# Joint semaphores for pairs of GpSimd and ScalarE pieces in a row maximum that ignores NaN

## The chip, the cores and the metric

The kernel runs on one NeuronCore of a Trainium2 chip. The metric is the device time of one execution in microseconds (us). The executions of one kernel in one set of rounds spread over 0.16 to 0.75 us here, so differences of half a us can be read if several runs are taken; each comparison with the kernel before uses runs of the same chip and rounds. All runs were with a granted clock (the share of full clock that the chip allows) of 1.00.

## The reference

The input is 32 x 2048 x 2048 floats, about a tenth of them NaN. The result is the maximum of each row of 2048, NaN left out.

```python
def reference(x, axis):          # axis = -1
    return np.nanmax(x, axis=axis).astype(np.float32)
```

That is 537 MB to read and 0.26 MB to write.

## The kernel before

The data flows through four stages. SyncE (SP) issues loads of a tile (7 rows of 2048 floats in each of 128 partitions) into one of three buffers `xt`. ScalarE (ACT) makes 16-bit keys `kt` of the upper halves of the floats. GpSimd (POOL) turns keys back into upper halves that are no longer NaN and writes them into `xt`; for some pieces ScalarE does this itself (a "back" piece, a negative number in the list of tiles). VectorE (DVE) takes the maximum of each row. When VectorE is done with a buffer, its next load is issued.

A tile's plan is a triple: sizes of loads, of pieces, and of reductions, in quarters of a row:

```python
    + [([28], [7, 9, 12], [16, 12])] * 7
    + [([28], [9, 12, -7], [8, 20])]          # the last 7 quarters are cleaned by ScalarE
...
    + [([4, 4, 3, 2, 4, 2, 3, 3, 3], [2, 2, 4, (-2.0, 1), 2, 3, 3, (-1, 2), (1, -1, 1), 2, -1.0], [4, 4, 4, 4, 4, 4, 4])]
```

There are 74 tiles. The order between engines is kept by hand. Each engine counts its instructions on one semaphore of its own; an instruction that depends on others waits for their counts. In this program an instruction carries one wait; each further one becomes an instruction of its own ahead of it:

```python
    def add(self, who, engine, issue, deps, lane=None, step=1):
        want = self.needed(who, deps)
        for s, v in want[:-1]:
            engine.wait_ge(self.sems[s], v)         # an instruction of its own
        inst = issue()
        for s, v in want[-1:]:
            inst._wait_ge(self.sems[s], v)          # on the instruction itself
        name = lane or who
        inst.then_inc(self.sem(name), step)
        self.count[name] += step
        event = (name, self.count[name])
        self.past[event] = {**self.seen[who], name: event[1]}
        return event
...
    e = dve([e for a, b, e in clean if b > lo and a < done] + part,
            nc.vector.tensor_reduce, ...)           # a row maximum: waits for POOL, or for POOL and ACT
```

A reduction whose quarters were cleaned partly by GpSimd and partly by ScalarE so has two waits: an instruction on VectorE's sequencer (EVENT_SEMAPHORE in the trace), then the reduction. VectorE has 18 such extra waits in the whole program, and the trace shows 18 EVENT_SEMAPHORE records just before reductions, of 21 ns each.

## Time and profile before

| | before |
|---|---|
| device time, median of 6 runs (range) | 1253.72 us (1253.66 to 1253.86) |
| DMA queue of the loads, share of 16 engines' span | 99.3% |
| VectorE, ScalarE, GpSimd busy | 89%, 79%, 93% |
| separate waits of VectorE before reductions | 18 |
| landing of the last load (its data complete) | 1243.20 us |

The prediction shows the lines that say what bounds the kernel.

The timeline of the tail before (start us, length us, engine, line, operation, count, idle time before it and who ended it):

```profile
1233.78 1.15 ACT L187 ACTIVATE kt<-xt,scalars 128x1024 uint16<-128x1024 int16 x1 [0.33 <-DMA xt<-in_x_dram]
1237.89 8.42 POOL L191 TENSOR_SCALAR xt<-kt 128x1536 int16<-128x1536 uint16 x6 [0.95 <-ACT kt L187]
1239.84 8.87 DVE L195 TENSOR_REDUCE acc<-xt 128x1 f32<-128x2048 f32 x4 [0.50 <-POOL xt L191]
```

Read it downwards: ScalarE waited 0.33 us for a load, GpSimd then 0.95 us for ScalarE, and VectorE 0.50 us for GpSimd. After that VectorE has four row maxima to do without a pause, and the end follows 12.0 us after 1239.84 us.

### The profile page before, as it was taken

How to read it: one execution, taken by the hardware profiler on the slowest of the kernel's cores; microseconds unless marked ns; L12 is line 12 of the kernel's file. 1: busy time of each engine (PE TensorE's matmuls, PEld its weight loads, DVE VectorE, ACT ScalarE, POOL GpSimd, SP SyncE). 2: the span in 40 equal slices, each digit the busy share in tenths (PEclk: the TensorE clock that was granted, in tenths of full speed). 3: DMA queues.
4: the chain of work that ended last, by engine and by line, in shares of the span. 5: the costliest groups of instructions: out<-in, count | busy, mean ns of one | idle time of the engine just before them, and what ended most of it. 6: DMA issues, size and time to landing. Idle time of an engine off the chain costs nothing.

```text
span 1251.8 us, 892 instructions
## 1 busy us (share of the span) xinstructions
DVE 1110.9 (89%) x181; ACT 986.9 (79%) x273; POOL 1168.4 (93%) x242
## 2 busy tenths in 40 slices
DVE  0788989888889988898988888998888899999998
ACT  3777887778787877788777877777777878999998
POOL 2999989998999899998999899999999999989997
DMA  9999999999999999999999999999999999999997
GB/s 415 436 418 436 440 440 436 422 433 440 440 434 423 433 440 440 436 425 429 440 440 438 425 427 440 440 438 429 423 440 440 435 434 421 437 428 431 431 428 288
DMA packets 15991, 537.20 MB, mean 429 GB/s; under 512 B 2544, under 2 KB 2544, under 8 KB 3568
## 3 DMA queue, kind: packets, MB, share of 16 engines
q1 hardware_dynamic: 15984, 537.14, 99.3%
q14 instruction: 7, 0.06, 0.0%
HBM read 536.87 MB, written 0.26 MB: 429 GB/s over the span
## 4 chain that ended last, share of the span: by engine, by line
DMA 36%; DVE 33%; POOL 19%; ACT 10%; SPq 1%; issue 1%; DVEq 0%
DMA xt<-in_x_dram 36%; DVE acc L195 33%; POOL xt L191 19%; ACT kt L187 9%; ACT xt L187 1%; SPq L253 1%; DVE none L201 0%; DVE acc L215 0%; SPq L411 0%; DVEq L124 0%; SPq L183 0%
## 5 line engine op out<-in xcount | busy, mean ns | idle before, releaser
L191 POOL TENSOR_SCALAR xt<-kt 128x3584 int16<-128x3584 uint16 (+11 forms) x236 | 1167.4, 4946 | 78.5 <-ACT kt L187 60.3
L195 DVE TENSOR_REDUCE acc<-xt 128x3 f32<-128x6144 f32 (+4 forms) x175 | 1107.7, 6380 | 137.1 <-POOL xt L191 129.2
L187 ACT ACTIVATE kt<-xt,scalars 128x3584 uint16<-128x3584 int16 (+9 forms) x247 | 935.5, 3825 | 257.8 <-DMA xt<-in_x_dram 241.8
L187 ACT ACTIVATE xt<-kt 128x512 int16<-128x512 uint16 (+6 forms) x24 | 52.8, 2200 | 0.7
L187 ACT ACT_TABLE_LOAD x1 | 1.3, 1283 | 0.9 <-SPq L183 0.9
L195 DVE TENSOR_REDUCE xt<-xt 128x1 f32<-128x1536 f32 x1 | 1.7, 1742 | 0.0
L221 DVE MEMSET scalars<- 128x1 f32 x1 | 0.1, 59 | 1.0 <-SPq L183 1.0
L201 DVE TENSOR_SCALAR none<-acc 128x414 int32<-128x414 f32 (+1 forms) x2 | 0.8, 380 | 0.1
L215 DVE TENSOR_TENSOR acc<-acc,none 128x414 int32<-128x414 int32 (+1 forms) x2 | 0.7, 374 | 0.1
L201 POOL TENSOR_SCALAR late<-acc 128x91 int32<-128x91 f32 x1 | 0.5, 545 | 0.1
L215 POOL TENSOR_TENSOR acc<-acc,late 128x91 int32<-128x91 int32 x1 | 0.3, 343 | 0.1
L397 POOL MEMSET const-float32-0.0<- 128x1 f32 x1 | 0.1, 98 | 0.2 <-issue 0.2
L187 ACT ACTIVATE scalars<-scalars 128x1 f32<-128x1 f32 x1 | 0.2, 203 | 0.0
L397 POOL MEMSET const-uint8-127<- 128x1 uint8 x1 | 0.1, 102 | 0.0
L397 POOL MEMSET const-bfloat16-1.0<- 128x1 bf16 x1 | 0.1, 101 | 0.0
L397 POOL MEMSET const-float32-1.0<- 128x1 f32 x1 | 0.1, 98 | 0.0
## 6 DMA issues: line engine op xcount, KB each, us to landing
xt<-in_x_dram SPq DMA_DIRECT2D x61, 7168.0 KB, 22.5
xt<-in_x_dram SPq DMA_DIRECT2D x2, 5120.0 KB, 17.3
xt<-in_x_dram SPq DMA_DIRECT2D x3, 2816.0 KB, 22.5
xt<-in_x_dram SPq DMA_DIRECT2D x4, 2048.0 KB, 22.1
xt<-in_x_dram SPq DMA_DIRECT2D x5, 1536.0 KB, 28.9
xt<-in_x_dram SPq DMA_DIRECT2D x2, 3584.0 KB, 24.5
xt<-in_x_dram SPq DMA_DIRECT2D x6, 1024.0 KB, 26.7
xt<-in_x_dram SPq DMA_DIRECT2D x3, 1792.0 KB, 29.8
```

The source lines that it names most:

```text
L187: return order.add("act", nc.scalar, lambda: nc.scalar.activation(**kw), deps)
L191: "pool", nc.gpsimd, lambda: nc.gpsimd.tensor_scalar(**kw), deps
L195: return order.add("dve", nc.vector, lambda: do(**kw), deps)
L201: lambda: engine.tensor_scalar(out=none, in0=acc, scalar1=NONE, scalar2=float(0x00800000), op0=ALU.is_equal, op1=ALU.mult,),
L215: lambda: engine.tensor_tensor(out=bits, in0=bits, in1=none, op=op),
L221: e_top = order.add("dve", nc.vector, lambda: nc.vector.memset(top, EDGE), [])
L253: lambda: nc.sync.dma_start(out=xt[:, at : at + c], in_=xg[:, base + at : base + at + c]),
L397: nc = _bacc.Bacc("TRN2", target_bir_lowering=False, num_devices=1)
```

## The change

The last GpSimd piece and the last ScalarE piece that one reduction needs now count on a semaphore of that pair. The reduction waits for the value 2 of it, in one wait on itself. The core of the diff:

```diff
+APART = (70, 71, 72, 73)                    # tiles left as they were
...
+def joints(pieces, reds):                   # which pieces form a pair of one reduction
+    ...
+    for need in needs:
+        if len(need) == 2 and all(sum(i in n for n in needs) == 1 for i in need):
+            for i in need:
+                pairs[i] = tuple(need)
+    return pairs
...
-    def add(self, who, engine, issue, deps, lane=None, step=1):
+    def add(self, who, engine, issue, deps, lane=None, step=1, joint=False):
...
-        self.past[event] = {**self.seen[who], name: event[1]}
+        past = self.past.get((name, event[1] - step), {}) if joint else {}
+        self.past[event] = {**past, **self.seen[who], name: event[1]}
...
-        def act(deps, **kw):
-            return order.add("act", nc.scalar, lambda: nc.scalar.activation(**kw), deps)
+        def act(deps, pair=None, **kw):
+            return order.add("act", nc.scalar, ..., deps, lane=pair, joint=pair is not None)
... (the same for pool)
+                pairs = {}
+                if number not in APART:
+                    pairs = joints(pieces, [n // Q for n in reds])
...
+                def name(i):
+                    return f"pair{number}_{pairs[i][0]}" if i in pairs else None
```

In the two programs every tile operation stands in the same place. VectorE has 10 separate waits fewer (tiles 9, 17, 25, 33, 41, 63, 66, 67, 68, and one in tile 74, the last), ScalarE has 4 more.

More of the change, by code (lines that the diff above doesn't have):

```diff
@@ L77, in total @@
     return sum(sum(map(abs, p)) if isinstance(p, tuple) else abs(p) for p in pieces)
+def joints(pieces, reds):
+    flat = []
+    at = 0
+    for step, parts in enumerate(pieces):
+        for c in parts if isinstance(parts, tuple) else (parts,):
+            flat.append((at, at + abs(c), c < 0, step + isinstance(c, float)))
+            at += abs(c)
+    needs = []
+    done = 0
+    for n in reds:
+        over = [i for i, (a, b, _, _) in enumerate(flat) if a < done + n and b > done]
+        done += n
+        pools = [i for i in over if not flat[i][2]]
+        backs = [i for i in over if flat[i][2]]
+        if pools and backs and flat[pools[-1]][3] > flat[backs[-1]][3]:
+            backs = []
+        needs.append(pools[-1:] + backs[-1:])
+    pairs = {}
[4 more added lines that the diff above has]
+    return pairs
 class Order:
@@ L184, with pool @@
         order = Order(nc)
-        def act(deps, **kw):
-            return order.add("act", nc.scalar, lambda: nc.scalar.activation(**kw), deps)
-        def pool(deps, **kw):
+        def act(deps, pair=None, **kw):
             return order.add(
-                "pool", nc.gpsimd, lambda: nc.gpsimd.tensor_scalar(**kw), deps
+                "act",
+                nc.scalar,
+                lambda: nc.scalar.activation(**kw),
+                deps,
+                lane=pair,
+                joint=pair is not None,
+            )
+        def pool(deps, pair=None, **kw):
+            return order.add(
+                "pool",
+                nc.gpsimd,
+                lambda: nc.gpsimd.tensor_scalar(**kw),
+                deps,
+                lane=pair,
+                joint=pair is not None,
             )
@@ L225, with last @@
         kfree = [[] for _ in range(NKEYS)]
+        clock = 0
+        def last(uses):
+            return list({back: e for back, _, e in sorted(uses, key=lambda u: u[1])}.values())
         key = 0
@@ L269, with cleaned @@
                 held = []
+                pairs = {}
+                if number not in APART:
+                    pairs = joints(pieces, [n // Q for n in reds])
+                flat = sum((p if isinstance(p, tuple) else (p,) for p in pieces), ())
+                half = {}
+                piece = 0
+                def cleaned(a, b, k, i, e):
+                    nonlocal clock
+                    clock += 1
+                    both = [(a, b, k, flat[i] < 0, clock)]
+                    if i in pairs:
+                        if pairs[i] not in half:
+                            half[pairs[i]] = both
+                            return
+                        both += half.pop(pairs[i])
+                    for a, b, k, back, when in both:
+                        kfree[k].append((back, when, e))
+                        clean.append((a, b, e))
+                def name(i):
+                    return f"pair{number}_{pairs[i][0]}" if i in pairs else None
                 def release():
-                    for a, b, k, kp, e in held:
+                    for a, b, k, kp, e, i in held:
                         e = act(
                             [e],
+                            name(i),
                             out=xt[:, a:b].bitcast(i16)[:, 1::2],
@@ L280, in release @@
                         )
-                        kfree[k].append(e)
-                        clean.append((a, b, e))
+                        cleaned(a, b, k, i, e)
                     held.clear()
@@ L292 @@
                         used = 0
-                        kold, kfree[key] = kfree[key], []
+                        kold, kfree[key] = last(kfree[key]), []
+                        assert all(k != key for q in half.values() for _, _, k, _, _ in q)
                         if at + c == sum(loads) * Q:
-                            kold = kold + kfree[(key + 1) % NKEYS]
+                            kold = kold + last(kfree[(key + 1) % NKEYS])
                     e_key = act(
@@ L313 @@
                         if back:
-                            held.append((at - c, at, key, kp, e_key))
+                            held.append((at - c, at, key, kp, e_key, piece))
                             if not wait or at == sum(loads) * Q:
@@ L319 @@
                                 [e_key],
+                                name(piece),
                                 out=to,
@@ L326 @@
                             )
-                            kfree[key].append(e)
-                            clean.append((at - c, at, e))
-                        while reds and done + reds[0] <= min([at] + [h[0] for h in held]):
+                            cleaned(at - c, at, key, piece, e)
+                        piece += 1
+                        open_ = [h[0] for h in held] + [p[0] for q in half.values() for p in q]
+                        while reds and done + reds[0] <= min([at] + open_):
                             n = reds.pop(0)
```

## The prediction

> **What bounds the kernel now.** I read the page's counts first (part 1), then the slices (part 2), then the chain that ended last, then single records of the trace around the reductions that have two waits.
>
> ```profile
> DVE 1110.9 (89%) x181; ACT 986.9 (79%) x273; POOL 1168.4 (93%) x242
> DMA  9999999999999999999999999999999999999997
> q1 hardware_dynamic: 15984, 537.14, 99.3%
> HBM read 536.87 MB, written 0.26 MB: 429 GB/s over the span
> ```
>
> No compute engine is full, although GpSimd (POOL) is near it. The DMA engines are: 99.3% of 16 engines' span, a 9 in every slice but the last. The busy-time view of stretches says the same without the start and the tail:
>
> ```profile
> 20.00:1236.00 1216.00, 1096.03 (x172) 973.26 (x261) 1155.96 (x229) 1.00 1.00 433
> 1040.00:1236.00 196.00, 195.51 (x52) 188.53 (x76) 184.23 (x55) 1.00 1.00 429
> 1236.00:1252.00 16.00, 12.53 (x8) 10.14 (x10) 9.84 (x9) 1.00 0.40 155
> ```
>
> (Columns: stretch, its length, DVE, ACT, POOL, clock, DMA share, GB/s.) From 20 to 1236 us the DMA share is 1.00 and 433 GB/s come in. From 1040 us VectorE is full as well, 195.51 of 196 us, so there I have to ask which of the two sets the end. The chain that ended last answers it:
>
> ```profile
> 1213.18 23.03 DMA xt<-in_x_dram
> 1236.21 0.03 issue
> 1236.24 1.58 ACT kt L187
> 1237.82 0.07 issue
> 1237.89 1.92 POOL xt L191
> 1239.81 0.03 issue
> 1239.84 2.01 DVE acc L195
> 1241.84 0.20 issue
> 1242.04 2.06 DVE acc L195
> 1244.10 0.13 issue
> 1244.23 2.15 DVE acc L195
> 1246.38 0.05 issue
> 1246.42 2.29 DVE acc L195
> ```
>
> (Start us, length us, what.) A load of 1 MB issued at 1213.18 lands 23.03 us later, though at 429 GB/s its own bytes take 2.4 us: it stands behind some 20 us of earlier loads. So its landing at 1236.21 is set by bytes and rate, not by the moment VectorE freed a buffer. After it come one key (ACT), one clean (POOL), four row maxima on VectorE, two tiny fix-ups and the store. The end is therefore **the stream, to 1236.2 us, plus a tail of 15.6 us** (1251.8 - 1236.2). A change of waits can only gain in that tail, or lose by letting the stream run dry.
>
> [...] the two-wait reductions have an EVENT_SEMAPHORE record on VectorE's sequencer just before them, the others have none. [...] Where POOL ended last and VectorE was ready, a one-wait reduction started 35 ns after POOL's end (1239.801 to 1239.836). A two-wait reduction, whose separate wait was POOL's, started 103, 103, 110 and 107 ns after (at 1065.339, 1140.913, 1237.048, 1246.424): 38 ns to the EVENT_SEMAPHORE, then about 70 ns for the instruction behind it. The price of the second wait, when the one that ends last is the separate one, is thus **about 70 ns**. [...]
>
> **The change part by part.** Comparing the order of instructions of the two programs, every tile operation stands in the same place with the same size; only waits differ. On VectorE 10 of 18 separate waits go: one each in tiles 9, 17, 25, 33, 41, 63, 66, 67, 68, and one in the last tile. Three other pairs of the last tile keep two waits, because a third piece of their row still counts on POOL's own semaphore (the pair's event does not carry POOL's earlier count). On ACT nothing is removed, and four keys (tiles 63, 66, 67, 68) now wait for POOL and for the pair: four separate waits added. Tiles 70 to 73 are left out by the list in the source.
>
> 1. *Tiles 9 to 41 (5 waits).* The reductions start at 158.50, 293.83, 429.06, 564.60, 699.86, each 32 to 33 ns after ScalarE's clean and 439 to 466 ns after POOL's. One line shows it:
>
> ```profile
> 158.50 10.82 DVE L195 TENSOR_REDUCE acc<-xt 128x5 f32<-128x10240 f32 x1 [1.54 <-ACT xt L187]
> ```
>
> The separate wait (POOL) had been over for 400 ns; the reduction sat at its own wait. Gain 0.
>
> 2. *Tiles 63, 66, 67, 68 (4 waits).* Back to back, reductions of VectorE start some 80 to 90 ns ahead of the recorded end of the one before. Those of tiles 66 and 67 (1110.625, 1125.678) start 90 and 87 ns before that end: full pace, gain 0. Those of 63 and 68 (1065.339, 1140.913) start 103 ns after POOL's end, and 68 and 33 ns after the previous reduction's end: gain about 70 ns each, 0.14 us together. But this frees buffers earlier in a stretch where the DMA share is 1.00, so it shortens a queue, not the stream. On the path: 0.
>
> 3. *Last tile.* The third row's reduction (1237.048) starts 38 ns before the previous end instead of 82: its early wait would now be an older piece (POOL ended it at 1235.522) and the pair's wait sits on the instruction, so it gains 45 ns. The next one waits 0.50 us for POOL anyway (1239.84), and swallows it. Of the last three, at 1242.039, 1244.231, 1246.424, each starts 82 to 84 ns before the recorded end of its predecessor, the back-to-back pace: start to start 2.19 us. Their separate waits opened inside that time. Even the last, where POOL and ACT both ended at 1246.317 and 107 ns passed, coincides with the pace to 1 or 2 ns. Gain on the path: 0 to 0.002 us.
>
> 4. *ACT's four added waits.* At some 60 to 70 ns each if they are the last to open, at most 0.28 us, spread over tiles at 1060 to 1150 us where ACT is busy 188.53 of 196 us; it has 7 us of slack there, and the load queue of 20 us lies beyond. On the path: 0.
>
> Sum: 0.00 us of the tail, 0.00 of the stream; **1253.66 us**, the median of before less the 2 ns.
>
> **Rivals.** (a) *Every removed wait counts*: 10 x 0.07 = 0.7 us, 1253.0 us. For it speaks that VectorE is full from 1040 us on; against it the records above, where only three of the ten or so waits cost anything, and the 20 us of queued loads. (b) *The tail gains*: if in other executions POOL or ACT ends the last rows a little later than in this one, up to 3 x 0.07 = 0.2 us of the four last reductions could be won, 1253.45 us; the last row stands right at the edge, so a few tens of ns are plausible. (c) *ACT's extra waits or the additional semaphores delay a key that feeds POOL*, and POOL comes late in the tail: at most 0.3 us, 1253.95 us; against it, the last tile has no added wait on ACT and ACT waited for DMA data at 1233.78 and 1236.24, so delays are wiped out there.
>
> **Range and chances.** The three runs of before lie within 0.20 us, and its profiled run took 1253.59. Rivals (b) and (c) are a few tenths either way, and another session may shift both kernels by some tenths: I take 1253.2 to 1254.0. Two per cent are 25 us. That would need the stream to slow or stop, and no wait here is worth more than a tenth of a us: same 0.99, 0.005 to either side.
>
> **What would show it right or wrong.** Right: DMA share 1.00 to 1236 us again, last landing at 1236.2 within some tenths, VectorE's last four reductions 2.19 us apart, the reductions at 1065 and 1141 starting about 35 ns after POOL's end and not 103, total idle of VectorE before reductions unchanged but for tenths. Wrong: a last landing that moves by over 0.5 us, an idle DMA stretch near the four changed keys, or a new gap between the last four reductions.

No term of the sum goes with them; it came to 0.00 us of the tail and 0.00 of the stream, so 1253.66 us. That the stream cannot bring more rests on the measured DMA share of 1.00, at 433 GB/s, alone; that 433 GB/s is its limit is not shown.

## More of the kernel before

One view is the DMA view of a short stretch. This is the one of 1231 to 1233 us, near the end of the stream of loads (queue and kind, then packets, MB, share of 16 engines):

```profile
q1 hardware_dynamic: 169, 0.86, 104.4%
q14 instruction: 1, 0.01, 1.0%
```

(A packet counts whole in the stretch in which it starts, so a share can pass 100%.) Queue 1 brings the data. Queue 14, labelled "instruction", is read here as the program itself.

## The result and the profile after

| | before | after |
|---|---|---|
| device time, median of 6 runs (range) | 1253.72 (1253.66 to 1253.86) | 1253.22 us (1253.08 to 1253.31) |
| recorded instructions | 892 | 886 |
| idle of VectorE before and between its last eight reductions | 0.50 us | 0 |
| last instruction fetch in the trace | 1231.70 us | 1245.68 us |

The ratio of the two is 0.9996, with a 95% interval from 0.9983 to 1.0009 (ratios are the mean time of one kernel's runs over that of the other's of the same rounds, so not quite the ratio of these medians). By that interval the kernels are the same within 2%, as forecast. That interval contains 1. But the ranges of the runs do not overlap, and they did not on the two later chips where both kernels ran: 16 runs of the changed kernel lie between 1253.07 and 1253.39, all 31 runs of the kernel before, in four sets of rounds, between 1253.44 and 1254.01. So there is a gain of about **0.5 us**, 0.04%, that the prediction's sum does not contain.

The parts of the page are all but the same:

```profile
span 1251.4 us, 886 instructions
DVE 1110.7 (89%) x181; ACT 986.6 (79%) x273; POOL 1168.6 (93%) x242
q1 hardware_dynamic: 15984, 537.14, 99.3%
```

The stretches, in the same columns as in the prediction, also: DMA share 1.00, 433 GB/s, and VectorE full from 1040 us.

```profile
20.00:1236.00 1216.00, 1095.74 (x172) 973.33 (x262) 1155.84 (x229) 1.00 1.00 433
1040.00:1236.00 196.00, 195.45 (x52) 188.82 (x77) 184.35 (x55) 1.00 1.00 429
```

And the line of tile 9, where the prediction saw no gain, answers as it should: the reduction still waits for ScalarE, and as long.

```profile
158.32 10.82 DVE L243 TENSOR_REDUCE acc<-xt 128x5 f32<-128x10240 f32 x1 [1.55 <-ACT xt L226]
```

The difference is in the tail. The timeline after:

```profile
1230.67 17.63 DVE L243 TENSOR_REDUCE acc<-xt 128x1 f32<-128x2048 f32 x8
1237.47 8.41 POOL L236 TENSOR_SCALAR xt<-kt 128x1536 int16<-128x1536 uint16 x6 [0.27 <-ACT kt L226]
```

VectorE now runs eight reductions without a pause; its 0.50 us of idle time is gone. So is ScalarE's wait for the load, and GpSimd waits 0.27 us instead of 0.95. The waits of the last tile did not do this: the load itself arrived earlier. The landings in the two traces show it (us; loads numbered from 0, the last is 104):

```
load            98        99       100       103       104
before     1231.77   1233.76   1236.21   1241.08   1243.20
after      1232.02   1233.27   1235.70   1240.66   1243.15
```

Up to load 98 the changed kernel is 0.25 us *later* (the times of one kernel's six runs spread over about as much, 0.20 us before and 0.23 us after). From 98 to 99 the kernel before takes 1.98 us, the changed one 1.24. The pause of 0.74 us before load 99 falls where its instruction packet stands, at 1231.70. In the changed kernel this stretch has no such packet:

```profile
q1 hardware_dynamic: 169, 0.87, 104.1%
```

It comes later, in the DMA view of 1233 to 1250 us, at 1245.68 by the trace, after the last load has landed:

```profile
q1 hardware_dynamic: 1523, 3.70, 54.8%
q14 instruction: 1, 0.01, 0.2%
```

In both traces VectorE had started 189 recorded instructions at that moment. With 10 instructions fewer, VectorE starts its 189th at 1244.50 us in place of 1230.42.

How do 0.74 us of a late load become 0.5 us of time? VectorE has some slack: in three traces with the packet before load 99 (before, and e1 and e3 below) the load is 0.74, 0.92 and 0.97 us late (against 1.24 us after load 98), and VectorE idles 0.50, 0.72 and 0.76 us. And more than this idle time cannot be won there, because without it VectorE works from 1141 us to the end with no pause over 0.04 us:

```profile
1141.21 80.59 DVE L243 TENSOR_REDUCE acc<-xt 128x3 f32<-128x6144 f32 x26
1221.71 1.75 DVE L243 TENSOR_REDUCE xt<-xt 128x1 f32<-128x1536 f32 x1
1223.49 24.81 DVE L243 TENSOR_REDUCE acc<-xt 128x1 f32<-128x513 f32 x12
```

The end of the changed kernel therefore no longer hangs on the last loads.

### The profile page after: what moved, and what is told of

Read it like the earlier page. It is cut to its first block, busy times and chain, and to the rows that moved or that the text cites. A ratio compares the mean times of both kernels' runs of the same rounds, so it can differ in the third digit from the quotient of the medians. Undisturbed runs are those within 1.5% of the kernel's fastest.

```text
span 1251.4 us, 886 instructions
## 1 busy us (share of the span) xinstructions
DVE 1110.7 (89%) x181; ACT 986.6 (79%) x273; POOL 1168.6 (93%) x242
## 3 DMA queue, kind: packets, MB, share of 16 engines
q1 hardware_dynamic: 15984, 537.14, 99.3%
## 4 chain that ended last, share of the span: by engine, by line
DMA 38%; DVE 29%; POOL 20%; ACT 12%; issue 1%; SPq 0%; ACTq 0%
DMA xt<-in_x_dram 38%; DVE acc L243 29%; POOL xt L236 20%; ACT kt L226 11%; ACT xt L226 1%; SPq L307 0%; DVE none L249 0%; DVE acc L263 0%; SPq L491 0%; ACTq L158 0%; SPq L219 0%
```

## The experiments

The theory after this comparison, the **fetch theory**: the removed waits gain nothing as waits. They gain as *instructions*: with fewer of them VectorE's next 8192 bytes of program are fetched behind the stream of loads instead of inside it. Rivals: the **wait theory** (one wait instead of two gains in the last tile) and the **buffer theory** (reductions of tiles 63 and 68 start earlier, free buffers earlier, and the stream gains). All experiments gave correct results.

### Parts of the change, alone

`e1`: pairs in the last tile only. `e2`: pairs in the nine earlier tiles only.

```diff
-APART = (70, 71, 72, 73)
+APART = tuple(range(1, 74))            # e1
+APART = (70, 71, 72, 73, 74)           # e2
```

> Pairs in the last tile alone; VectorE has 1 separate wait fewer than before, ScalarE none more. Fetch theory (the 0.5 us come from an 8192-byte instruction fetch of VectorE that moved from 1231.7 us, inside the stream of loads, to 1245.7 us, behind it, because VectorE has 10 instructions fewer): the fetch comes back to some 1231 to 1240 us and the time is about 1253.6. If the fetch has moved to 1237 or later by that one instruction, part of the gain stays. Wait theory (the gain is the cheaper wait in the last rows): 1253.2.

> Pairs in the nine earlier tiles, none in the last tile; VectorE has 9 separate waits fewer, ScalarE 4 more. Fetch theory: fetch at 1240 us or later, time 1253.2 to 1253.3. Wait theory: the last tile's waits are those of before, so 1253.7. Buffer theory (buffers freed earlier in tiles 63 and 68 speed the stream): 1253.2.

On one chip, kernel before 1253.62 us (7 runs): e1 took **1253.90** (1253.61 to 1254.04, 4 runs), e2 **1252.94** (1252.82 to 1253.08, 4 runs). The part with the last tile's cheaper waits gains nothing; the part without them has the whole gain. The wait theory has fallen. (Both times lie some 0.3 us outside what the fetch theory expected, e1 above and e2 below. In e1's profiled run, its slowest, load 99 is later than in the kernel before, and VectorE idles 0.72 us; for e2 see e9.) In e1 the fetch stands at 1231.96 us and load 99 lands 2.16 us after load 98; in e2 the fetch stands at 1246.76, load 99 follows after 1.24 us, and VectorE's last eight reductions have no idle time.

### The instructions back, with nothing else

`e3`: the changed kernel, with all its pairs, plus ten waits on VectorE for a count reached long before, one in each of tiles 43 to 52, where VectorE has idle time (in the kernel before it is busy for 16.5 to 18.3 of each 20 us from 720 to 900 us). `e4`: the same ten in the kernel before.

```diff
                             n = reds.pop(0)
+                            if done == 0 and 43 <= number < 53:
+                                nc.vector.wait_ge(order.sems["dve"], 1)
```

> The changed kernel with all its pairs and ten waits put into VectorE's stream, one in each of tiles 43 to 52, each on a count reached long before, where VectorE idles anyway. Fetch theory: VectorE's count of instructions is that of before again, the fetch is back near 1231.7 us and the time near 1253.65. Wait theory and buffer theory: all pairs are there, 1253.2.

> The kernel before with the same ten waits added. Fetch theory: the fetch comes ten instructions earlier, near 1205 us, still in the stream; time 1253.5 to 1254.0 if a fetch anywhere in the stream delays all later landings, about 1253.2 to 1253.4 if it only hurts among the last few loads. Wait and buffer theory: 1253.7.

Same chip and rounds: e3 took **1253.68** us (1253.62 to 1253.78, 4 runs), the level of the kernel before; e2, which has the pairs of the nine earlier tiles and no idle waits, took 1252.94. (The changed kernel itself was not run on this chip.) Its DMA view of 1231 to 1233 us has the packet again (the trace says 1232.04),

```profile
q1 hardware_dynamic: 167, 0.87, 105.5%
q14 instruction: 1, 0.01, 1.0%
```

and its tail has the old waits again:

```profile
1233.97 1.15 ACT L226 ACTIVATE kt<-xt,scalars 128x1024 uint16<-128x1024 int16 x1 [0.53 <-DMA xt<-in_x_dram]
1238.07 8.42 POOL L236 TENSOR_SCALAR xt<-kt 128x1536 int16<-128x1536 uint16 x6 [1.14 <-ACT kt L226]
1240.01 8.87 DVE L243 TENSOR_REDUCE acc<-xt 128x1 f32<-128x2048 f32 x4 [0.76 <-POOL xt L236]
```

The ten waits cost nothing by themselves: up to load 98 the landings of e3 are 0.29 us earlier than in the changed kernel. Load 99 then lands 2.21 us after 98. This undoes the gain while every pair stays, which neither rival allows.

e4 took **1253.69** us (1253.54 to 1254.29, 4 runs). Its fetch came earlier, at 1218.59 us (the expectation had said near 1205), and so did the pause: loads 91 to 92 now take 3.22 us instead of 2.43 in the changed kernel, and loads 98 to 99 only 1.24. A fetch 13 us earlier in the stream therefore costs about the same: counted from load 91, loads 92 to 103 stay 0.6 to 0.8 us later than in the changed kernel. Only the very last load catches up.

### A part that opens no wait earlier

`e5`: pairs in tiles 9, 17, 25, 33 and 41 only. The prediction showed that their separate waits had opened 400 ns before; ScalarE gets no extra wait here.

```diff
-APART = (70, 71, 72, 73)
+APART = tuple(range(60, 75))
```

> Pairs in tiles 9, 17, 25, 33 and 41 alone: five of VectorE's separate waits fewer, none of which had opened last, and no wait added anywhere. Fetch theory: the fetch goes to about 1242 us or later, so the whole gain is there, 1252.9 to 1253.3. Wait theory and buffer theory: 1253.65, as not one reduction starts earlier by it.

`e6`: the changed kernel with five idle waits on VectorE (`43 <= number < 48` in the edit of e3).

> The changed kernel with five of the ten idle waits put back on VectorE (tiles 43 to 47). Fetch theory: the fetch request falls at about 1236 to 1239 us, so it delays at most the last two to four loads: 1253.1 to 1253.6, between the two kernels. Wait and buffer theory: 1253.2.

`e7`: the changed kernel with ten idle waits on SP, in the same tiles:

```diff
                 at = 0
+                if 43 <= number < 53:
+                    nc.sync.wait_ge(order.sems["dve"], 1)
                 for c in loads:
```

> The changed kernel with ten such waits on the queue engine (SP) in place of VectorE, in the same tiles. Fetch theory, with VectorE's own count as the cause: VectorE's fetch stays at about 1245 us, 1253.2. If any ten instructions on any engine do it: 1253.65.

`e8`: the changed kernel, unedited, on the same chip.

> The changed kernel itself on this chip, to compare e5 to e7 with it in the same rounds: 1253.1 to 1253.25 by every theory. e5 may come out below it by up to 0.3 us if the four waits added on ScalarE cost something.

The four ran in the same rounds; the kernel before took 1253.71 us (1253.44 to 1254.01, 9 runs).

| run | VectorE's wait instructions, against before | time, us (5 runs each) | last fetch, us |
|---|---|---|---|
| e5 | -5 | 1253.36 (1253.06 to 1253.43) | 1243.11 |
| e6 | -5 | 1253.42 (1253.25 to 1253.86) | 1239.74 |
| e7 | -10, SP +10 | 1253.24 (1253.16 to 1253.42) | 1245.88 |
| e8 | -10 | 1253.16 (1253.11 to 1253.32) | 1245.63 |

e5 has most of the gain, 0.35 us, although not one of its reductions starts earlier by its pair; its runs and those of the kernel before just miss each other (1253.43 and 1253.44). Its fetch falls 0.09 us before the last load lands, and VectorE has no idle time in the tail. Its time lies 0.06 us above the range expected and 0.20 above e8; why is not shown. This is against the buffer theory as well. e6 is between, as expected, and its runs overlap those of the kernel before: its fetch falls before the last two landings, load 103 lands 2.68 us after 102 (1.84 in the changed kernel), and the profiled execution, its slowest with 1253.86 us, ends on that load. The chain that ended last starts there:

```profile
1220.31 21.42 DMA xt<-in_x_dram
1241.74 0.02 issue
1241.76 1.58 ACT kt L226
```

e7 separates the engines. Ten instructions more on SP leave the time and VectorE's fetch as they are. They move another packet, from 1130 us to 1055 us: in both traces SP had then started 80 or 81 recorded instructions. So the last packet follows VectorE's count, and this one SP's.

One packet does not follow so simple a rule. In the kernel before, e1 and e4 it comes at 434 us; in every run without the five early waits it comes at 386 us, although VectorE has fewer instructions ahead of it (47 started in the changed kernel, 56 in the kernel before). Why is not shown. Tile 25's separate wait opens at 428.64 us in the kernel before, 5.6 us ahead of the packet; no run tests whether the two are connected. This packet is not the cause of the gain: in e3 it stands at 386 us as in the changed kernel, and the gain is gone.

### Is there a better version?

`e9`: e2 again. `e10`: the changed kernel again. `e11`: pairs in tiles 9 to 41 and in the last, so that ScalarE gets no extra wait (`APART = (63, 66, 67, 68, 70, 71, 72, 73)`).

> Pairs in the nine earlier tiles, none in the last, once more, beside the changed kernel in the same rounds. It was 0.68 us under the kernel before where the changed kernel was 0.50 under it, but on two chips. Fetch theory: the two have the fetch behind the stream alike, so they lie within 0.2 us of each other. If the pairs of the last tile cost something, this one is 0.2 us or more below.

> The changed kernel on this chip: 1253.1 to 1253.3 by every theory.

> Pairs in tiles 9 to 41 and the last tile: six separate waits fewer on VectorE, none added on ScalarE. Fetch theory: the fetch comes at about 1242 to 1245 us, behind all loads that the end hangs on: 1253.0 to 1253.3. If the four waits added on ScalarE in the changed kernel cost time, this one lies below it.

Kernel before 1253.72 us (1253.54 to 1253.86, 9 runs). e9 took 1253.19 (1253.06 to 1253.61), e10 1253.17 (1253.07 to 1253.39), e11 1253.16 us (1252.99 to 1253.39), 5 runs each: no difference. The larger gain of e2 in the first set, 0.68 us, did not come again on this chip, where e9 gains 0.53. The four waits added on ScalarE cost nothing that shows, and no version was found that beats the changed kernel.

## Why the prediction was right or wrong

The time, 1253.22 us, lies just inside the stated range, 1253.2 to 1254.0, and "within 2%" was right. The point given, 1253.66 us, was 0.44 us too high. That the range still held was luck: its tenths were meant for rivals (b) and (c) and for a shift between sessions, none of which happened. Of its own signs, two of being right came true (the reductions at 1065 and 1141 us start 34 and 32 ns after GpSimd's end, and the last four start 2.19 us apart), and one of being wrong did by a hair: the landing that it called the last moved by over 0.5 us, from 1236.21 to 1235.70. By its steps:

- **What bounds the kernel**: right for the kernel before. The DMA share and the rate are the same after, but in the changed kernel's trace the end hangs on VectorE, which no longer waits. One sentence of it was wrong: that the landing at 1236.21 us "is set by bytes and rate". It was also not the last landing: loads come in until 1243.20 us. Of the time to that landing, 0.74 us were set by one packet of program. The prediction read the page's "q14" share of 0.0% as nothing. Over the whole span it is nothing; it counts by where it stands.
- **The price of a second wait, about 70 ns**: it held. (Of its four records the one at 1246.424 says little, because that start coincides with the back-to-back pace, as its part 3 notes.) In tile 68 of the changed kernel the reduction starts 32 ns after GpSimd's end (1141.178 to 1141.210) and not 103.
- **Part 1 (tiles 9 to 41, gain 0)**: this is the step that failed. As waits they gain 0, as forecast: the reduction still starts when ScalarE ends. But the step priced a wait only by what it delays, and each is also an instruction. Taking those five away alone moved the fetch to the end of the last load and gave 0.35 us (e5).
- **Part 2 (tiles 63 to 68, nothing on the path)**: right as far as can be seen. As VectorE of the changed kernel no longer pauses after 1141 us, 0.07 us saved there could now count; e11, without these pairs, is as fast as e10, so it is too small for these runs.
- **Part 3 (the last tile, 0 to 2 ns)**: right about the waits: with them alone the time did not fall (e1). Wrong about the 0.50 us of idle time that "swallows" a gain, which it took as given. It was the price of the fetch and is what the change removed.
- **Part 4 (ScalarE's added waits)**: right, e11 without them is not faster. (Its 60 to 70 ns agree with the trace of before: where a separate wait of ScalarE opened last, as at 1152.475 us, the key behind it started 62 ns later.)
- **Rivals**: (a) named 1253.0 us and (b) 1253.45 us, each within 0.23 us of the result and nearer than the point given, but neither reason was the reason: in e3 every removed wait that (a) counts stays removed and the gain is gone, and e1 has (b)'s cheaper waits in the tail and gains nothing. (c) did not come about. None of the three rivals held the true one.

What is shown and what is argued: that the time follows the place of VectorE's fetch is shown by e1 to e7, in both directions and with the waits kept apart. How a packet of 309 ns makes loads 0.74 us late is an estimate from the trace: the next two slow packets, of 4096 bytes, start at 1232.00 and 1232.35 us and took 368 and 487 ns in place of the usual 159, so 309 + 209 + 328 = 0.85 us if all three went through one DMA engine; the load was 0.74 us late. e1 and e3 have the same two slow packets (368 or 373, and 487 ns); the changed kernel has none. The fetches in the middle of the stream show jumps of landings too, 0.26 to 0.74 us at the packets near 255, 386 and 434 us in the traces of before, e1 to e4 and the changed kernel, with one of 0.11. At those near 940 and 999 us the jumps are 0 to 0.37 us. Why the size varies stays open; the trace as kept does not say which of the 16 engines carried a packet.

VectorE itself works on across the fetch: in the kernel before, its four reductions from 1230.42 to 1239.33 us run without a pause across the packet at 1231.70. It was the load behind the packet that came late, by 0.74 us. The prediction did not look there.

That the last packet is VectorE's is a conclusion from the counts and from e3 and e7: all these packets are labelled q14, and the trace names no engine. All seven inside the span are of 8192 bytes in both traces. Two pairs of them lie about 128 recorded instructions of one engine apart (GpSimd at 52 and 180 started instructions, ScalarE at 48 and 175); giving these to GpSimd and ScalarE is an estimate by the counts alone.

## What to carry to other kernels

In this kernel, whose loads took 99.3% of the 16 DMA engines' span, the program was a load too: ten waits fewer moved an instruction fetch from 1231.70 to 1245.68 us, and that one fetch among the last loads cost about 0.5 us where a wait cost about 0.07. When, in a kernel like this, a small change of waits or of bookkeeping gives or takes some tenths of a us that no wait accounts for, look at the instruction queue's packets in the DMA view of the tail before and after. And test it as here: put idle instructions on the same engine, far from the place in question, and see whether the time follows their number.
